# Weights of the third late gate requested inside the last scan; sample operands built before the last chunk

## The chip, the cores and the metric

The kernel runs on one core of one Trainium2 chip. The metric is the device time of one execution in microseconds. The core has a matrix engine (PE, with its own weight loads, PEld), a vector engine (DVE), an activation engine (ACT), a general engine (POOL) and a queue that issues transfers (SP). Each engine takes its instructions in a fixed order; they wait for each other by semaphores.

## The reference

One decoder layer on 1024 prompt tokens and 8 x 8 sample tokens, model width 1024, all in 32-bit floats. In short:

```python
h = rmsnorm(x, g_mix_pre) * (1 + scale_m) + shift_m
sc_b, sc_c, sc_x, z, xbc, dt_raw = split(h @ w_in)   # z: columns 3072..4095, the gates
y_sc = sc_b * causal_dwconv(sc_c * sc_x)             # short convolution
xs, Bm, Cm = split(silu(causal_dwconv(xbc)))
y_ssd, new_state = ssd_scan(xs, dt, A, Bm, Cm, d_skip, ssm_state)   # 4 groups of 4 heads
y_ssd = rmsnorm((y_ssd * silu(z)) per group) * ssm_norm_g
x = x + gate_m * rmsnorm(concat(y_sc, y_ssd) @ w_out)
x = x + gate_f * rmsnorm(swiglu(x))
```

The scan works on the prompt in chunks of 128 tokens with a state that is carried on. The 64 sample tokens start from a state given for each of their 8 sequences (state_ssm) and return a new one.

## The kernel before, in words

Every product is made of three: each operand is split into a high part (an ACT cast, `copy`) and a low part (a DVE subtraction), and high x high, high x low and low x high are summed (lines 332 to 334 in `acc3`). A weight block is loaded into a `raw` tile, split into `wh` and `wl`, and used as the stationary operand against the hidden rows `hh` (high) and `hl` (low) in three column chunks of 384, 384 and 320 tokens.

The mixer goes over the four groups g = 0..3. `ssd(g)` is a generator that makes the scan of a group in four double chunks: `part_a` (transposes, products B x C), `part_m` (decay factors), `part_b` (lines 739 to 769: products, the state S carried on DVE in lines 760 and 763, and the products with S in line 754). After the fourth it does the sample tokens: `sample_a` (factors), `sample_states` (load and transpose the given states, s0), `sample_b` (lines 810 to 822: the operands XS and BS of the state products), and, for the two head pairs, products from s0, the state products XS x BS (line 873), the update of s0 in place (lines 874 and 877), and its transfer out (line 878). `merge` interleaves a scan with side work: in scans 0 to 2 the input projections of the next group and the conditioning products, in scan 3 `gate` and `norm` of groups 0 and 1 (lines 888 and 901). The program order is only a priority: the compiler's scheduler lets later instructions run ahead when it thinks them ready, and fixes the order of each engine.

Behind the loop the memory on the left side is given up (`left.close()`, line 1092) and divided anew. The new pools lie on the old ones in this order: `rws` (4 raw tiles) on `rawp`, the first four tiles of `wsc` (weight parts) on `wp`, the other four and the sums `x56` on `fmp` (8 tiles of all 1088 tokens) and on `stp` (6 small tiles). A new tile waits for the old ones under it. `gate_late(2)` and `gate_late(3)` (line 1140) are the gates of groups 2 and 3, with weights from `plain_w` (lines 1009 to 1015 load and split). Between their chunks a generator `sums_h` makes the operand sums (lines 1117 to 1125, DVE) that the short-convolution projections (`sc_unit`, lines 1030 to 1070) need; `sums_last` follows. `raw_half` asks for weights in line 1010, the older `load_w` in line 301; both on SP. `y_out` (lines 935 and 936) sends finished rows out on SP too.

`rawp` has four tiles. In scan 3 they hold the two raw halves of gate 0, the two of gate 1, and then, in the first two again, s0 of the two head pairs.

Of the kernel before, what the change touches and what calls it, by code (L numbers as in the profile page):

```python
# [10 lines left out]
F32R = mybir.dt.float32r  # L11
# [5 lines left out]
P = 128  # L17
D = 1024
KT = 8
# [14 lines left out]
def hymba_step(ctx, tc, i, o):  # L34
# [7 lines left out]
    base, mid, left, right, banks = (ExitStack() for _ in range(5))  # L42

    def pool(stage, name, bufs, **kw):
        return stage.enter_context(tc.tile_pool(name=name, bufs=bufs, reuse_waits="tile", **kw))
# [21 lines left out]
    def fm(dt=F32):  # L67
        return fmp.tile([P, T], dt, tag="fm", name=nm("fm"))
# [8 lines left out]
    def st(shape, dt=F32):  # L77
        return stp.tile(shape, dt, tag="st", name=nm("st"))

    def gz(shape):  # L80
        return gzp.tile(shape, F32, tag="gz", name=nm("gz"))
# [39 lines left out]
    w_in = i["w_in"][0]  # L121
# [565 lines left out]
    def ssd(g, x0, x1, Bf, Cf):  # L687
# [4 lines left out]
        def part_a(j):  # L692
            cc = slice(2 * j, 2 * j + 2)
            col = 256 * j
            tpx, tpb = pz(), pz()
            for c in range(2):
                oc = col + c * P
                for p in range(2):
                    nc.tensor.transpose(tpx[:, c * 256 + p * P:c * 256 + (p + 1) * P], xc[p][:, oc:oc + P], ident)
                nc.tensor.transpose(tpb[:, c * P:(c + 1) * P], Bf[:, oc:oc + P], ident)  # L700
            for c in range(2):
                oc = col + c * P
                mm(tpb[:, 256 + c * P:256 + (c + 1) * P], Bf[:, oc:oc + P], Cf[:, oc:oc + P], start=True, stop=True)
            xd = st([P, 2, 2, 4, 64])
            for e, factor in enumerate((dt, edend)):
                nc.vector.tensor_tensor(xd[:, e], tpx.rearrange("p (c r q) -> p c r q", c=2, r=4),
                                        bc(factor[:, cc, hs], 3, 64), op=mult)
            bb = st([P, 2, 2, P])
            nc.scalar.copy(bb[:, 0].rearrange("p c n -> p (c n)"), tpb[:, :256])
            nc.vector.tensor_tensor(bb[:, 1], tpb[:, 256:].rearrange("p (c n) -> p c n", c=2),  # L710
                                    bc(ut, 1, 2), op=mult)
            return xd, bb
# [61 lines left out]
        def sample_a():  # L774
            tpx, tpb = pz(), pz()
            for p in range(2):
                nc.tensor.transpose(tpx[:NS, p * P:(p + 1) * P], xc[p][:, col:], ident)
            nc.tensor.transpose(tpb[:NS, 0:P], Bf[:, col:], ident)
            mm(tpb[:NS, P:P + NS], Bf[:, col:], Cf[:, col:], start=True, stop=True)
            ac = pz()  # L780
            for r in range(4):
                mm(ac[:, r * NS:(r + 1) * NS], sel(4 * g + r), acT[:, col:], start=True, stop=True)
            xd = st([NS, 2, 4, 64])
            for e, factor in enumerate((dt, edend)):
                nc.vector.tensor_tensor(xd[:, e], tpx[:NS, :256].rearrange("p (r q) -> p r q", r=4),
                                        bc(factor[:NS, 8, hs], 2, 64), op=mult)
            EC = st([P, 3, 4, NS])
            acv = ac[:, :256].rearrange("p (r l) -> p r l", r=4)
            E, Cx = EC[:NS, 0], EC[:, 1]
            nc.scalar.activation(Cx, acv, AF.Exp)  # L790
            nc.vector.tensor_tensor(E, acv[:NS], bc(acum[:NS, 8, hs], 2, NS), op=sub)
            nc.vector.tensor_scalar(E, E, 0.0, None, op0=mn)
            nc.scalar.activation(E, E, AF.Exp)
            CBm = EC[:NS, 2, 0, :]
            nc.vector.tensor_tensor(CBm, tpb[:NS, P:P + NS], utsf, op=mult)

            XB = gzp.tile([96, 768], F32R, tag="gz", name=nm("XB"))
            Bp = XB[:NS, 512:768].rearrange("k (j n) -> k j n", j=2)
            nc.scalar.copy(Bp[:, 0, :], tpb[:NS, 0:P])
            nc.vector.tensor_tensor(Bp[:, 1, :], tpb[:NS, 0:P], Bp[:, 0, :], op=sub)  # L800
            nc.vector.tensor_tensor(E, E, bc(CBm, 1, 4), op=mult)
            dsm = sp.tile([P, 2, 8], F32, tag="dsm", name=nm("dsm"))
            for p in range(2):
                for h in range(2):
                    nc.vector.tensor_copy(dsm[64 * h:64 * h + 64, p, :],
                                          bt(Cx[64 * h:64 * h + 64, 2 * p + h, :])[:, :, 7])
            nc.vector.tensor_tensor(Cx, Cx, bc(Cf[:, col:], 1, 4), op=mult)
            return xd, E, Cx, XB, Bp, dsm

        def sample_b(xd, XB, Bp):  # L810
            XS = XB[:, 0:512].rearrange("k (q m) -> k q m", q=2)
            BS = st([96, 2, 512], F32R)
            for q in range(2):
                own, other = slice(32 * q, 32 * q + 32), slice(32 - 32 * q, 64 - 32 * q)
                v = xd[own, 1].rearrange("k r q -> k (r q)")
                nc.scalar.copy(XS[own, q, :], v)
                nc.scalar.copy(XS[64:96, q, :], v)
                nc.vector.tensor_tensor(XS[other, q, :], v, XS[own, q, :], op=sub)
                for part, at in ((0, own), (0, other), (1, slice(64, 96))):
                    (nc.vector if part else nc.gpsimd).tensor_tensor(  # L820
                        BS[at, q, :].rearrange("k (b n) -> k b n", b=4), bc(Bp[own, part, :], 1, 4),
                        bc(blk4[own], 2, P), op=mult)
            return XS, BS

# [13 lines left out]
        m = part_m(0, *a)  # L838
        yield
        for j in range(4):  # L840
            a2 = part_a(j + 1) if j < 3 else sample_a()
            yield
            part_b(j, *a, *m)
            yield
            if j < 3:
                a = a2
                m = part_m(j + 1, *a)
                yield
        xd, E, Cx, XB, Bp, dsm = a2
        s0, s0T = sample_states(0)  # L850
        XS, BS = sample_b(xd, XB, Bp)
        yield
        S = state[0]
        fps = pz()
# [31 lines left out]
    def gate(g, y):  # L886
        ws = load_cols(w_in, 3072 + 256 * g, 2)
        for m in range(2):
            for c in range(3):
                proj_c(ws[m], hh, hl, gate_out(y[m]), c)  # L890
                yield
# [64 lines left out]
    def blend(a, b, na, nb):  # L956
# [4 lines left out]
        yield from a  # L961
        yield from b

    tl = [[] for _ in range(4)]
    run(group_tiles(0, tl[0]))
    for g in range(4):
        if g < 3:
            side = group_tiles(g + 1, tl[g + 1])
            if g > 0:
                side = blend(side, ada_steps(g), 12, 9)  # L970
        else:
            side = itertools.chain(*(f for h in range(2) for f in (
                gate(h, tl[h][:2]), norm(h, tl[h][:2], lambda: gz([P, 2, 384]), fm_row))))
        run(merge(ssd(g, *tl[g]), side, (0.67, 1.17, 1.17, 1.67)[g]))
    pre_scale("A_f", 4, gpre1)
    ys = [t[:2] for t in tl]
# [64 lines left out]
    def plain_w(w, cols):  # L1041
        raws = [raw_half(w, j, cols) for j in range(2)]
        W = {}
        for m in range(2):
            for j in range(2):
                t = in_turn(w_from).tile([P, 2, 4, P], F32R, tag="wc", name=nm("wp_"))
                part(t[:, 0], t[:, 1], raws[j][:, :, m * P:(m + 1) * P])
                W[m, j] = [[t[:, s, k] for k in range(4)] for s in range(2)]
        return W
# [40 lines left out]


    left.close()
    rws, wsc = pool(left, "rws", 4), pool(left, "wsc", 8)
    x56, x4 = pool(left, "x56", 8), pool(left, "x4", 4)
    pap, psx, psy = (pool(left, n, b) for n, b in (("pap", 2), ("psx", 1), ("psy", 1)))
    raw_from, w_from = [rws] * 4, [wsc] * 8

    X_sc = [{p: [] for p in (4, 5, 6)} for _ in SQ]
    X_t = {p: [] for p in (4, 5, 6)}
# [40 lines left out]
    def gate_late(g, y, W, between):  # L1140
        n_ = 0
        for m in range(2):
            w = [W[m, j][s][k] for s in range(2) for j in range(2) for k in range(4)]
            for c, (c0, n) in enumerate(CH):
                ps = pm()
                chained(acc3, ps, n, [(w[k], w[8 + k], hh[k][:, c0:c0 + n], hl[k][:, c0:c0 + n]) for k in range(KT)])
                gate_out(y[m])(ps, c, c0, n)
                for gen in between.get(n_, ()):
                    next(gen, None)
                n_ += 1  # L1150
# [6 lines left out]

    sums = sums_h()
    norm2, norm3 = (norm(g, ys[g], sq_row, sx_row) for g in (2, 3))
    gate_late(2, ys[2], plain_w(w_in, 3072 + 512), {n: [sums] for n in range(6)})  # L1160
    gate_late(3, ys[3], plain_w(w_in, 3072 + 768), {n: [sums] for n in range(6)})
    run(sums)
    sums_last()

# [560 lines left out]
```

## Time and profile before

| | us |
|---|---|
| median of 3 runs (1778.58 to 1783.43) | 1783.38 |
| the profiled execution | 1773.94 |
| its span | 1772.2 |
| PE busy in it | 1688.8 (95%) |
| DVE busy | 1174.1 (66%) |
| ACT busy | 778.6 (44%) |

A profile row gives times in microseconds from the span's start. A row of a timeline holds the start, the time taken by the run of like instructions, the engine, the line, the operation, output <- inputs, the shape and, in brackets, how long the engine was idle before it and what ended that. Matmuls are pipelined, so the rate of a stream of them is read from start to start. A row of a table of stretches holds the stretch and its length, then each engine's busy time with its count of instructions, the granted PE clock (1.00 is 2.4 GHz, 0.50 is 1.2 GHz), the busy share of the DMA engines and what they moved.

### The profile page before, as it was taken

Reading aid. Unit: us, or ns where it says so; the run is one execution under the profiler, and the core shown is the slowest. Engines: PE = TensorE matmul, PEld = TensorE weight load, DVE = VectorE, ACT = ScalarE, POOL = GpSimd, SP = SyncE. Lnnn points to the kernel's source line nnn. Section 1 sums busy time; section 2 is a strip of 40 time slices with the busy share of each in tenths; the row PEclk is TensorE's granted clock in tenths of the full one; section 3 lists DMA queues with packets and bytes.
Section 4 is the critical chain, followed back from the end, with each engine's and each line's share of the span. In section 5 each row is a group of like instructions: output and inputs, shape, how many; then the busy total and the mean of one; then the engine's idle time right before and its main releaser. Section 6 shows DMA issues by size and latency. Waiting matters only on the chain.

```text
span 1772.2 us, 31608 instructions
## 1 busy us (share of the span) xinstructions
PE 1688.8 (95%) x12624; PEld 1602.8 (90%) x12624; DVE 1174.1 (66%) x2263; ACT 778.6 (44%) x1597; POOL 237.6 (13%) x333
## 2 busy tenths in 40 slices
PE   5999999999699999999999899999999999899997
PEld 4998887889599899998989899999999999899987
DVE  5588777767867776660127769666665576677845
ACT  3456454558334333331226666444444455322303
POOL 2111021200000000000000000122222200322303
PEclk9999999999699999999999999999999999999999
DMA  9210435331502412348275634334434448856243
GB/s 316 70 36 25 129 119 177 119 122 52 172 25 87 149 50 98 115 137 301 84 247 181 195 115 147 120 137 148 147 137 152 146 151 311 324 213 236 99 152 119
DMA packets 160634, 259.74 MB, mean 147 GB/s; under 512 B 10561, under 2 KB 124401, under 8 KB 158182
## 3 DMA queue, kind: packets, MB, share of 16 engines
q1 hardware_dynamic: 160486, 257.71, 42.3%
q8 instruction: 99, 1.62, 0.4%
q14 instruction: 49, 0.40, 0.1%
HBM read 186.30 MB, written 71.38 MB: 145 GB/s over the span
## 4 chain that ended last, share of the span: by engine, by line
PE 82%; DVE 7%; DMA 3%; ACT 3%; issue 2%; POOL 1%; SPq 1%; DVEq 0%; POOLq 0%; ACTq 0%
PE pm L332 10%; PE pm L333 10%; PE pm L334 10%; PE pz L1055 7%; PE pz L1053 7%; PE pz L1054 7%; PE pm L1053 7%; PE pm L1055 7%; PE pm L1054 7%; DMA raw<-in_w_in 1%; PE pz L749 1%; PE pm L207 1%; PE pz L743 1%; PE pz L754 1%; PE pz L721 1%
## 5 line engine op out<-in xcount | busy, mean ns | idle before, releaser
L310 DVE TENSOR_TENSOR wl<-raw,wh 128x512 fp32r<-128x512 f32 (+1 forms) x83 | 59.0, 733 | 102.0 <-ACT wh L309 98.8
L334 PE MATMUL pm<-hb,wl 128*128 128x512 f32 (+2 forms) x320 | 108.3, 340 | 3.2 <-DVE wl L310 3.2
L333 PE MATMUL pm<-hb,wh 128*128 128x512 f32 (+2 forms) x320 | 108.1, 339 | 0.0
L332 PE MATMUL pm<-hb,wh 128*128 128x512 f32 (+2 forms) x320 | 106.8, 339 | 1.1 <-ACT wh L309 1.0
L333 PE MATMUL pm<-h,wh 128*128 128x384 f32 (+1 forms) x306 | 101.8, 333 | 0.0
L332 PE MATMUL pm<-h,wh 128*128 128x384 f32 (+1 forms) x306 | 101.5, 332 | 0.0
L334 PE MATMUL pm<-h,wl 128*128 128x384 f32 (+1 forms) x306 | 100.9, 331 | 0.0
L309 ACT CAST wh<-raw 128x512 fp32r<-128x512 f32 (+1 forms) x85 | 54.0, 667 | 106.1 <-PE pm L333 66.6
L1015 DVE TENSOR_TENSOR fs<-f,fs 128x512 fp32r<-128x512 f32 (+1 forms) x80 | 55.9, 711 | 27.5 <-ACT fs L1014 26.7
L334 PEld LDWEIGHTS pm<-hb,wl 128*128 128x128 f32 x320 | 61.2, 191 | 9.3 <-DVE wl L310 3.9
L1014 ACT CAST fs<-f 128x512 fp32r<-128x512 f32 (+1 forms) x80 | 46.7, 598 | 50.3 <-DMA f_d<-fs 33.0
L332 PEld LDWEIGHTS pm<-hb,wh 128*128 128x128 f32 x320 | 60.8, 191 | 7.0 <-ACT wh L309 1.6
L1070 DVE TENSOR_TENSOR facc<-facc,pz 128x288 f32<-128x288 f32 x124 | 55.9, 451 | 15.6 <-PE pz L1055 15.2
L333 PEld LDWEIGHTS pm<-hb,wh 128*128 128x128 f32 x320 | 61.1, 191 | 5.4
L332 PEld LDWEIGHTS pm<-h,wh 128*128 128x128 f32 x306 | 57.5, 188 | 1.3 <-issue 0.7
L333 PEld LDWEIGHTS pm<-h,wh 128*128 128x128 f32 x306 | 57.4, 188 | 1.0 <-issue 0.3
L334 PEld LDWEIGHTS pm<-h,wl 128*128 128x128 f32 x306 | 57.5, 188 | 0.9 <-issue 0.9
L1070 DVE TENSOR_TENSOR facc<-facc,pm 128x256 f32<-128x256 f32 x124 | 51.5, 415 | 5.7 <-PE pm L1055 4.5
L1032 POOL TENSOR_TENSOR raw<-raw 128x512 f32<-128x512 f32 x16 | 22.5, 1404 | 205.7 <-DVE raw L1030 205.7
L332 PE MATMUL pm<-bt,wh 128*128 128x384 f32 (+1 forms) x134 | 46.6, 347 | 0.0
L434 ACT COPY ext<-pm 128x384 f32<-128x384 f32 (+1 forms) x44 | 19.3, 445 | 57.9 <-PE pm L334 54.0
L333 PE MATMUL pm<-bt,wh 128*128 128x384 f32 (+1 forms) x134 | 43.7, 326 | 0.0
(7553 smaller groups left out, 6506.3 us busy)
## 6 DMA issues: line engine op xcount, KB each, us to landing
raw<-in_w_in SPq DMA_DIRECT2D x48, 512.0 KB
fc<-f_d SPq DMA_DIRECT2D x9, 2016.0 KB
f_d<-fs SPq DMA_DIRECT2D x31, 576.0 KB
wa<-in_w_ada SPq DMA_DIRECT2D x32, 512.0 KB
raw<-in_w_out SPq DMA_DIRECT2D x32, 512.0 KB
fc<-f_d SPq DMA_DIRECT2D x9, 1792.0 KB
f_d<-fs SPq DMA_DIRECT2D x31, 512.0 KB
raw<-in_w_gate SPq DMA_DIRECT2D x28, 512.0 KB
```

What stands on the lines that cost most here:

```text
L309: (nc.gpsimd.tensor_copy if hi_eng else nc.scalar.copy)(wh, raw)
L310: (eng or nc.vector).tensor_tensor(wl, raw, wh, op=sub)
L332: mm(ps[:, :n], wh, xh, start=(first and j == 0), stop=False)
L333: mm(ps[:, :n], wh, xl, start=False, stop=False)
L334: mm(ps[:, :n], wl, xh, start=False, stop=(last and j == end))
L1014: nc.scalar.copy(hi, v)
L1015: (eng or nc.vector).tensor_tensor(lo, v, hi, op=sub)
L1032: eng.tensor_tensor(a21, a11, a21, op=sub)
L1053: mm(ps, W[0][k], X[0][k], start=(start and k == 0), stop=False, skip_group_check=True)
L1054: mm(ps, W[0][k], X[1][k], start=False, stop=False, skip_group_check=True)
L1055: mm(ps, W[1][k], X[0][k], start=False, stop=(stop and k == nk - 1), skip_group_check=True)
L1070: nc.vector.tensor_tensor(out(q, i, h), out(q, i, h), ps, op=add)
```

## The change

In every scan the operands XS and BS of the sample tokens (`sample_b`) are built right behind `sample_a`, ahead of the fourth `part_b` instead of behind it, and BS lies in the `fm` pool instead of the `st` pool. In scan 3 a step `load_next` is put between the gate and the norm of group 1: it asks for the weights of the third gate, columns 3584 to 3839 of `w_in`, by `load_cols`, into two `raw` tiles and the two pairs `wh`, `wl` that the gates 0 and 1 use. `gate_late(2)` takes these. The eight tiles of `wsc` become two pools of four, and the ring of weight tiles now begins with the four on `fmp`; the fourth gate is the first to take from it.

```diff
@@ sample_b
-            BS = st([96, 2, 512], F32R)
+            BS = fm(F32R)[:96, :1024].rearrange("k (q n) -> k q n", q=2)
@@ ssd
-            a2 = part_a(j + 1) if j < 3 else sample_a()
+            if j < 3:
+                a2 = part_a(j + 1)
+            else:
+                a2 = sample_a()
+                XS, BS = sample_b(a2[0], *a2[3:5])
             yield
             part_b(j, *a, *m)
...
         s0, s0T = sample_states(0)
-        XS, BS = sample_b(xd, XB, Bp)
@@ the loop over the groups
+    w_next = []
+    def load_next():
+        w_next.extend(load_cols(w_in, 3072 + 512, 2))
+        yield
...
-            side = itertools.chain(*(f for h in range(2) for f in (
-                gate(h, tl[h][:2]), norm(h, tl[h][:2], lambda: gz([P, 2, 384]), fm_row))))
+            gates, norms = zip(*((gate(h, tl[h][:2]), norm(h, tl[h][:2], lambda: gz([P, 2, 384]), fm_row))
+                                 for h in range(2)))
+            side = itertools.chain(gates[0], norms[0], gates[1], load_next(), norms[1])
@@ behind left.close()
-    rws, wsc = pool(left, "rws", 4), pool(left, "wsc", 8)
+    rws, wsca, wscb = pool(left, "rws", 4), pool(left, "wsca", 4), pool(left, "wscb", 4)
-    raw_from, w_from = [rws] * 4, [wsc] * 8
+    raw_from, w_from = [rws] * 4, [wscb] * 4 + [wsca] * 4
@@ the late gates
-    gate_late(2, ys[2], plain_w(w_in, 3072 + 512), {n: [sums] for n in range(6)})
+    gate_late(2, ys[2], [[v[:, k] for v in w for k in range(KT)] for w in w_next], {n: [sums] for n in range(6)})
```

`gate_late(3)` keeps `plain_w`, with its list of parts now made by the caller.

## Rows read from the trace of the kernel before

**Rows 1.** The page: PE and its granted clock in 40 slices, in tenths.
```profile
PE   5999999999699999999999899999999999899997
PEclk9999999999699999999999999999999999999999
```

**Rows 2.** Table of stretches, end of scan 3 to the end of the late gates.
```profile
420.00:442.00 22.00, 22.00 (x171) 19.86 (x170) 17.50 (x38) 21.18 (x36) 4.00 (x4) 1.00 0.26 103
442.00:453.00 11.00, 10.39 (x112) 8.65 (x110) 7.68 (x16) 4.24 (x9) 0.46 (x2) 0.76 0.04 13
446.00:448.00 2.00, 2.00 (x21) 1.75 (x18) 1.90 (x4) 0.59 (x1) 0.00 (x0) 0.91 0.22 66
453.00:461.00 8.00, 5.03 (x20) 4.34 (x20) 5.71 (x18) 0.30 (x1) 0.00 (x0) 0.50 0.21 66
461.00:474.00 13.00, 0.00 (x0) 0.00 (x0) 12.98 (x16) 4.29 (x7) 0.00 (x0) 0.63 0.88 292
474.00:500.00 26.00, 25.96 (x144) 25.74 (x145) 25.32 (x38) 13.43 (x24) 0.00 (x0) 0.92 0.39 123
500.00:524.00 24.00, 24.00 (x147) 24.00 (x146) 9.70 (x17) 5.84 (x11) 0.00 (x0) 1.00 0.08 23
```

**Rows 3.** Waits of PE from 100 to 480: who for whom, total, times, longest.
```profile
PE pm L332 <- ACT wp__625_4819 L1014: 13.1, 1, 13.1
PE pz L873 <- DVE st L858: 4.4, 2, 2.2
PE pz L754 <- DVE S L763: 1.7, 1, 1.7
```

**Rows 4.** Chain that ended last, from 461 to 474: start, length, what.
```profile
461.12 1.21 DVE s L877 x2
462.35 4.12 DMA out_ssm_s<-s
466.52 6.82 DMA raw<-in_w_in
```

**Rows 5.** Timeline of SP, from 371 to 422: its issues in scan 3.
```profile
371.58 6.11 SPq L827 DMA_DIRECT2D s<-in_state_ssm  x2
421.77 1.34 SPq L935 DMA_DIRECT2D y_d<-nr  x2
```

**Rows 6.** Timeline of PE: the same matmuls at full and at half clock.
```profile
413.57 0.83 PE L289 MATMUL pz<-ident,sm 128*128 128x128 f32 x6
455.90 4.18 PE L289 MATMUL pz<-ident,sm 128*128 128x128 f32 x18 [2.97 <-DVE sm L283]
```

**Rows 7.** Timeline of ACT and DVE: the fourth gate's splits, and the last operand sum.
```profile
477.80 0.62 ACT L1014 CAST wp__654_5038<-raw 128x512 fp32r<-128x512 f32 x1 [0.70 <-DMA raw<-in_w_in]
480.47 0.68 DVE L1015 TENSOR_TENSOR wp__654_5038<-raw,wp__654_5038 128x512 fp32r<-128x512 f32 x1
535.62 0.72 DVE L1015 TENSOR_TENSOR h<-t,h 128x544 fp32r<-128x544 f32 x1
```

**Rows 8.** Timelines of ACT, DVE, POOL, PE in scan 1: XS, BS and their user.
```profile
249.55 0.40 ACT L816 CAST XB<-st 32x256 fp32r<-32x256 f32 x1
254.85 0.84 DVE L818 TENSOR_TENSOR XB<-st,XB 32x256 fp32r<-32x256 f32 x2
257.91 5.80 POOL L820 TENSOR_TENSOR st<-XB,blk 32x512 fp32r<-32x512 f32 x3
262.75 1.05 DVE L427 SCALAR_TENSOR_TENSOR fm<-ext,vT,fm 128x64 f32<-128x64 f32 x1
266.01 1.38 DVE L820 TENSOR_TENSOR st<-XB,blk 32x512 fp32r<-32x512 f32 x2
267.99 0.47 PE L873 MATMUL pz<-st,XB 96*128 96x512 f32 x1 [2.22 <-DVE st L858]
```

**Rows 9.** Timeline of DVE in scan 3: the state's update without and beside POOL.
```profile
427.82 0.42 DVE L760 TENSOR_TENSOR S<-S,ecd 128x256 f32<-128x256 f32 x1
438.15 0.98 DVE L760 TENSOR_TENSOR S<-S,ecd 128x256 f32<-128x256 f32 x1 [0.58 <-PE pz L754]
```

More of the change, by code (lines that the diff above doesn't have):

```diff
@@ L1142, in gate_late @@
         for m in range(2):
-            w = [W[m, j][s][k] for s in range(2) for j in range(2) for k in range(4)]
+            w = W[m]
             for c, (c0, n) in enumerate(CH):
@@ L1159, in hymba_step @@
     norm2, norm3 = (norm(g, ys[g], sq_row, sx_row) for g in (2, 3))
-    gate_late(2, ys[2], plain_w(w_in, 3072 + 512), {n: [sums] for n in range(6)})
-    gate_late(3, ys[3], plain_w(w_in, 3072 + 768), {n: [sums] for n in range(6)})
+    gate_late(2, ys[2], [[v[:, k] for v in w for k in range(KT)] for w in w_next], {n: [sums] for n in range(6)})
+    W = plain_w(w_in, 3072 + 768)
+    gate_late(3, ys[3], [[W[m, j][s][k] for s in range(2) for j in range(2) for k in range(4)] for m in range(2)],
+              {n: [sums] for n in range(6)})
     run(sums)
```

## The prediction

> **What bounds the kernel now.** Read the slices first [rows 1]: PE is busy nine tenths or more nearly everywhere, so PE bounds the kernel, and time is to be had only where PE stands still or runs at half clock. One slice in the middle shows 6 on both lines, and it is the place of the change. The table of stretches resolves it [rows 2]: PE is full up to 442 (22.00 of 22.00), then idle for 0.61 us up to 453, 2.97 up to 461 and 13.00 up to 474, and nearly full behind it (25.96 of 26.00). That is 16.6 us, and from 446 on the clock falls to 1.2 GHz. The table of PE's waits names the causes [rows 3]: 13.1 us for the first split weights of the third gate, and 4.4 us in two pieces for the state products of the sample tokens (line 873). The chain gives the first wait its history [rows 4]: the last update of s0 ends at 462.3, its transfer out takes 4.12 us, and only then is the weight request issued, which lands 6.82 us later. So the weights wait for a memory slot: their raw tile lies on s0 of the second head pair.
>
> **The weights, step by step.** The new request goes into raw tiles that gate 0 and gate 1 leave, and s0 of the second pair moves to the last raw half of gate 1. In SP's order these three issues stand between the loads of s0 at 371 and the first transfer of `y_out` at 421 [rows 5], 44 us in which SP only waits: neither the request nor s0, whose user comes behind 442, is late, and nothing is held behind them. The parts lie in `wh` and `wl`: the first half is free when gate 1's first half has been multiplied, the second when PE ends gate 1 at 442. In work nothing is added: four casts, four subtractions and two transfers of 512 KB leave `plain_w` and come back in `load_cols`. Where they go matters. The first half's two casts (2 x 0.62 us) and two subtractions (2 x 0.68 us) [rows 7] fall into 420 to 442, where ACT is busy 21.18 of 22 us and DVE 17.50 [rows 2]. So I expect that half at about 445. This suffices, because PE has the transposes and small products of the tail to do from 442 on.
>
> Between 442 and the end of the third gate PE then does the same work without the holes. Idle time removed: 0.61 + 2.97 + 13.00 = 16.6 us [rows 2]. Clock: the 18 matmuls of line 289 take 4.18 us at half clock against 3 x 0.8 = 2.4 for three sixes at full clock, 1.8 us [rows 6]; the 144 matmuls of the third gate take 25.96 us, at the rate of the fourth gate (24.00 / 147 = 0.163 us) they take 23.5, another 2.4 us [rows 2]. The ceiling is 16.6 + 1.8 + 2.4 = 20.8 us. From it I take 3 us for what I can't see: about 1.2 for the two casts in the full ACT stretch, the rest for an order of PE that is fixed ahead and doesn't meet the real moments. Term: **-17.8 us**. Its bounds: the ceiling of 20.8, and 13.1 [rows 3] if PE's order leaves the tail as it is and only the wait goes.
>
> **What is late next.** The fourth gate would start at about 480 instead of 500. The second quarter of its parts is cast by 478.4 and subtracted by 481.2 now [rows 7], behind the third gate's four splits, which no longer stand there (4 x 0.6 = 2.4 us): 479, so no wait. Its raw tiles now lie on s0 of the first pair and on the early weights, both done before s0 of the second pair. Then DVE: it is busy 7.68 + 5.71 + 12.98 + 25.32 = 51.7 of 58 us from 442 to 500, then 9.70 of 24 [rows 2], and the last operand sum of the next projection ends at 535.62 + 0.72 = 536.3 [rows 7]. Of the 61.4 us of DVE work between 442 and the fourth gate's end at 524, some 4 (splits and parts of `sample_b`) move ahead of 442; 57 us must fit into the 62 us up to 504. It fits with about 5 us to spare; so no term of its own, but a loss of up to 8 us is kept as a rival.
>
> **The operands, step by step.** In scan 1 POOL's multiplications of BS begin at 257.9 and DVE's two only at 266.0, behind the whole convolution of the next group's tile, so PE waits 2.22 us for line 873 [rows 8]; the second piece of the 4.4 us is the same in scan 2 [rows 3]. XS is ready at 255.7. Built behind `sample_a`, ahead of `part_b`, all of it is done some 10 us sooner, and PE is next held there by nothing that the rows show: -4.4 us. Against it: DVE's four instructions (0.84 + 1.38 = 2.2 us) and ACT's four casts (4 x 0.40 = 1.6 us) [rows 8] now stand in front of `part_b`, with its state updates queued behind DVE's. In scan 0, where line 754 already waits 1.7 us for the state [rows 3], I take 1 us more (bounds 0 and 2.2); in the others PE has projections at hand, so 0 (bound 2.2 each). BS in `fm` gives a small tile back to the chunk loop and takes one of eight large ones: in scan 3 the others are acT, the tiles of B and C, two y tiles and two norm rows, eight of eight; the y tiles and rows go free with the transfers of 421 [rows 5], long before norm 1 wants rows. I cost it at nothing; the cover is gone if those transfers are late. Term: -4.4 + 1.0 = **-3.4 us**, bounds -4.4 and 4 x 2.2 - 4.4 = +4.4.
>
> POOL and DVE disturb each other here: the state update of line 760 takes 0.42 us alone and 0.98 while POOL builds BS [rows 9]. The Trainium skill (SBUF — State Buffer, section "SBUF: two separate sides") gives a reason: a GpSimd instruction and a DVE instruction with two SBUF inputs take the same port pair by an exclusive lock, and the later one stands still. It speaks against this change, which puts more of POOL's work beside the state updates; the row at 438.15 agrees. By it, three more updates stretched by 0.56 us in each of four scans would cost 6.7 us if PE always waited for them, and the second term would turn to +3.3.
>
> **The sum.** -17.8 - 3.4 = -21.2 us against the profiled execution's 1773.94 gives 1752.7. That execution is 9.4 us below the median of the runs shown, so against the median of 1783.38 the forecast is **1762.2 us**. Differences under 0.3% (5.3 us) can't be told from no change.
>
> **Rivals.**
> *PE's order stays.* The third gate's products are queued behind the tail, because the order was fixed with the weights thought late; only the 13.1 us go: 1783.4 - 13.1 - 3.4 = 1766.9. For it: the order is fixed ahead. Against: nothing of the tail feeds these products. Chance 0.14.
> *DVE becomes the bound.* The sums end up to 8 us late, seen as idle PE at 505 to 520: 1770.2. For it: 51.7 of 58 us busy [rows 2]. Against: from 500 to 524 it has 14 us free. Chance 0.14.
> *The change doesn't do what it says.* The wait moves to the fourth gate: its request stays behind the transfers of `y_out` in SP's order and lands a whole landing of 6.8 us [rows 4] behind the 481 of now, 2 us of which were to spare at best: 1762.2 + 6.8 + 2 = 1771. Chance 0.05.
> *No change: the clock.* It began to fall from 446 to 448 while PE was busy 2.00 of 2.00 us with small products [rows 2]. If it stays at 1.2 GHz for the whole third gate, that takes 23.5 us more than at full clock: 1783.4 - 16.6 - 2.4 + 23.5 - 3.4 = 1784.5. Against: from 420 to 442, where the chunk's small products stand among full ones, it is 1.00. Chance 0.05.
> *Slower.* The pulled-up operands hold the state chain: `part_b` stands behind POOL's run of 5.8 us and the 2.2 + 1.6 us of DVE and ACT [rows 8], 9.6 us in each of four scans, 38.4 us: 1783.4 - 17.8 - 4.4 + 38.4 = 1799.6. It decides from 22.2 / 4 = 5.6 us a scan. Against: `part_b` reads nothing that POOL makes, and PE has side work. Chance 0.05.
> The forecast itself holds 0.57.
>
> **How the numbers follow.** Faster by over 0.3%: 0.57 + 0.14 + 0.14 + 0.05 = 0.90, less 0.05 for the spread of the runs (1778.58 to 1783.43): 0.85. Slower by over 0.3%: 0.05, and 0.01 for the spread: 0.06. Within: 0.09. The range goes from the ceiling, 1783.4 - 20.8 - 4.4 = 1758.2, less 3.7 of spread, 1754.5, to the latest of the faster rivals, 1771, plus 4.5, 1775.5.
>
> **What will show it.** Right: no wait of line 332 for split weights at 461 to 474; the third gate's matmuls stand among lines 832, 867 and 906 from about 445; the fourth gate starts near 480; the clock stays near 1.00; the two waits of line 873 are gone; the instruction counts of DVE and ACT are unchanged. Wrong: idle PE ahead of the fourth gate (its weights), at 505 to 520 (DVE) or at line 754 (the state chain); a clock of 0.50 through the third gate. The prediction fails as a whole if PE's idle time in the chunk loop grows by more than what the end of scan 3 loses.

## The result, and the profile after

| | before | after |
|---|---|---|
| median of 4 runs each, side by side (us) | 1783.37 | 1763.29 |
| range of the runs (us) | 1778.58 to 1783.43 | 1760.32 to 1764.89 |
| ratio, 95% interval | | 0.9892 (0.987 to 0.9914) |
| the profiled execution (us) | 1773.94 | 1764.2 |
| its span (us) | 1772.2 | 1762.5 |

The forecast was 1762.2 us (0.9881 of before), and the time fell on it. The two profiled executions differ by only 9.7 us, though, where the sum said 21.2. A second comparison of the same two kernels, below, gave 0.992 (0.9896 to 0.9944). The first question is therefore where the expected gain stands in the trace, and where it is lost again. Of all timed runs below one, of v_pool, is left out as a slow execution (2057.96 us at a granted clock of 0.749).

Table of stretches of the kernel after, over the same stretches as [rows 2], then one longer stretch. Columns as there: the stretch and its length, busy time of PE, PEld, DVE, ACT, POOL, granted clock, share and rate of the DMA engines.

```profile
442.00:453.00 11.00, 9.62 (x89) 8.99 (x90) 8.75 (x17) 4.82 (x10) 0.15 (x1) 0.84 0.04 12
453.00:461.00 8.00, 8.00 (x59) 6.67 (x59) 3.36 (x10) 1.17 (x2) 0.00 (x0) 0.63 0.22 66
461.00:474.00 13.00, 13.00 (x83) 12.62 (x82) 9.72 (x20) 3.42 (x5) 0.00 (x0) 0.97 0.30 104
474.00:500.00 26.00, 25.09 (x150) 24.56 (x149) 25.62 (x37) 11.83 (x22) 0.00 (x0) 1.00 0.54 177
500.00:524.00 24.00, 23.57 (x168) 23.18 (x166) 23.65 (x41) 11.67 (x23) 0.00 (x0) 1.00 0.15 44
...
470.00:526.00 56.00, 54.14 (x353) 53.19 (x352) 55.26 (x84) 27.30 (x51) 0.00 (x0) 1.00 0.39 125
```

The hole of 13.00 us is gone. Two things took part of its place. PE is full from 453 to 461 but at a granted clock of 0.63. And DVE is busy 55.26 of 56.00 us from 470 to 526: it has become the engine that is never free.

Waits of PE in the kernel after, in all and longest, first from 100 to 480, then from 480 to 660 (lines 754, 763 and 289 are the old ones; 1024 and 1025 are the old 1014 and 1015, 1063 to 1065 the old 1053 to 1055, 1078 the old 1068, 1127 the old 1117).

```profile
PE pz L754 <- DVE S L763: 4.5, 2, 2.8
...
PE pm L1063 <- ACT y L1078: 1.9, 1, 1.9
PE pz L289 <- DVE sm L283: 1.4, 1, 1.4
PE pm L1065 <- DVE w__726_5815 L1025: 0.9, 1, 0.9
PE pm L334 <- DVE wp__653_5038 L1025: 0.9, 1, 0.9
PE pm L1064 <- DVE h L1025: 0.5, 1, 0.5
PE pm L1063 <- ACT h L1024: 0.4, 1, 0.4
```

Of [rows 3] the 13.1 us and the 4.4 us are gone. The wait for the state (line 754) grew from 1.7 to 4.5 us: 2.8 in scan 0, where it was 1.7, and a new one of 1.7 in scan 3 (at 443.4). Behind 480 the kernel before has only these two:

```profile
PE pm L1053 <- ACT y L1068: 2.2, 2, 1.8
PE pz L289 <- DVE sm L283: 1.4, 1, 1.4
```

So the first two rows behind 480 are old. New are the four others, of 0.4 to 0.9 us, three of which end with a low half from DVE.

To place the difference, the same matmul is looked up in both traces, and its starts are compared:

| from, to | forecast (us) | measured (us) |
|---|---|---|
| start of the span, scan 0 reached | 0 | +3.1 |
| scan 0 | +1.0 | +2.6 |
| scans 1 and 2 | -4.4 | -4.7 |
| scan 3, up to the fourth gate's first product | -17.8 | -16.4 |
| fourth gate and first six projection units | 0 | +5.5 |
| the rest, to the end | 0 | +0.1 |
| sum | -21.2 | -9.7 |

The third and fourth lines are nearly right. The loss behind the fourth gate's start is the step that the sum lacked. From scan 0 on, start to start, this pair of traces gains 12.8 us.

For every kernel below two stretches are read: scan 3's start to the fourth gate's first product, and from there to the seventh projection unit. PE's idle time is the length less PE's busy time. The cost of the clock is the sum, over 48 equal slices of a stretch, of PE's busy time times one less the granted clock.

| kernel | first stretch | idle | clock | second stretch | idle | clock |
|---|---|---|---|---|---|---|
| before | 131.78 | 16.62 | 7.23 | 163.43 | 3.57 | 0.00 |
| after | 115.34 | 1.71 | 5.09 | 168.91 | 6.42 | 1.71 |
| after_again | 115.43 | 1.71 | 5.12 | 168.96 | 6.47 | 1.60 |
| weights_only | 115.44 | 0.73 | 6.81 | 173.78 | 9.93 | 2.98 |
| fm_late | 112.94 | 1.70 | 3.41 | 174.56 | 9.19 | 4.91 |
| early12 | 110.88 | 0.75 | 1.71 | 175.16 | 10.08 | 4.45 |
| v_act | 115.23 | 1.77 | 5.14 | 166.25 | 4.73 | 1.39 |
| v_pool | 115.16 | 1.78 | 5.11 | 171.59 | 9.40 | 2.15 |
| early123 | 112.45 | 1.77 | 1.71 | 169.19 | 6.65 | 1.52 |
| early123_again | 115.12 | 1.71 | 5.11 | 167.79 | 6.80 | 0.00 |
| low_pool | 110.80 | 1.71 | 0.00 | 172.60 | 8.98 | 2.70 |

What is left when idle time and clock are taken off is the same work in all of them: 107.8 to 109.1 us in the first stretch, 159.8 to 161.0 in the second. So the difference between these kernels in the two stretches is, to within 1.3 us in each, PE's idle time and PE's clock.

### The profile page after: what moved, and what is told of

Its sections match the earlier page's. It is cut to its first block, busy times and chain, and to the rows that moved or that the text cites. A ratio compares the mean times of both kernels' runs of the same rounds, so it can differ in the third digit from the quotient of the medians.

```text
span 1762.5 us, 31586 instructions
## 1 busy us (share of the span) xinstructions
PE 1693.1 (96%) x12624; PEld 1605.9 (91%) x12624; DVE 1173.0 (67%) x2263; ACT 773.5 (44%) x1595; POOL 231.8 (13%) x333
## 5 line engine op out<-in xcount | busy, mean ns | idle before, releaser
L333 PE MATMUL pm<-h,wh 128*128 128x384 f32 (+1 forms) x342 | 115.2, 337 | 0.0
L332 PE MATMUL pm<-h,wh 128*128 128x384 f32 (+1 forms) x342 | 115.1, 337 | 0.0
L334 PE MATMUL pm<-h,wl 128*128 128x384 f32 (+1 forms) x342 | 114.4, 336 | 0.0
L332 PEld LDWEIGHTS pm<-h,wh 128*128 128x128 f32 x342 | 65.5, 192 | 1.9 <-issue 1.0
L1080 DVE TENSOR_TENSOR facc<-facc,pz 128x288 f32<-128x288 f32 x124 | 55.9, 451 | 16.7 <-PE pz L1065 16.4
L333 PEld LDWEIGHTS pm<-h,wh 128*128 128x128 f32 x342 | 65.4, 191 | 1.1 <-issue 0.3
L334 PEld LDWEIGHTS pm<-h,wl 128*128 128x128 f32 x342 | 65.4, 191 | 0.9 <-issue 0.9
L332 PE MATMUL pm<-bt,wh 128*128 128x384 f32 (+1 forms) x146 | 51.4, 352 | 0.0
L334 PE MATMUL pm<-bt,wl 128*128 128x384 f32 (+1 forms) x146 | 48.5, 332 | 0.3 <-DVE wl L310 0.2
L333 PE MATMUL pm<-bt,wh 128*128 128x384 f32 (+1 forms) x146 | 48.1, 330 | 0.0
```

Source lines behind the costliest of these rows:

```text
L332: mm(ps[:, :n], wh, xh, start=(first and j == 0), stop=False)
L333: mm(ps[:, :n], wh, xl, start=False, stop=False)
L334: mm(ps[:, :n], wl, xh, start=False, stop=(last and j == end))
L1080: nc.vector.tensor_tensor(out(q, i, h), out(q, i, h), ps, op=add)
```

## The experiments

Three sets were run, each beside its own runs of the kernel before, whose medians were 1776.52 (14 runs), 1780.72 (13) and 1777.52 us (9); times of different sets are compared by their ratio to these. A trace is one execution, and not always a typical one: after_again, early12 and v_act were profiled in the slowest of their runs, early123, fm_late and low_pool in the fastest.

**The two kernels again.** No edit.

> The kernel before, unchanged, for a second profile. The first profiled execution took 1773.94 us, below every timed run (1778.58 to 1783.43). If executions differ by what the transfers at the start do, the second profile differs from the first by up to 8 us and mostly before 100 us of the span; the end of scan 3 should repeat: a PE wait of about 13 us for the third gate's split weights, two waits of 2.2 us in line 873. If the first profile was typical, the second lies within 2 us of it.

> The changed kernel, unchanged, for a second profile and more times. First profile 1764.2 us. Ratio 0.988 to 0.990. If the 3.2 us that the first profile was late before scan 0 are chance, they differ here; the 2.6 us lost in scan 0, the 4.6 us won in scans 1 and 2, and the 15 us won at the end of scan 3 should repeat within 0.5 us.

Measured: before 1776.98 us, span 1775.3; after 1761.74 us (1757.69 to 1765.59), span 1763.9, ratio 0.992 (0.9896 to 0.9944). Against the first trace of before, scan 0's +2.6, the -4.7 in scans 1 and 2 and the end of scan 3 (-16.4) repeat to within 0.2 us. The second trace of before differs in scan 1, which takes 89.6 us instead of 88.1: behind the 2.2 us wait of line 873 its granted clock falls, and it does so in other_slots too. A stretch of before_again:

```profile
268.00:272.20 4.20, 4.20 (x16) 4.07 (x15) 3.27 (x4) 0.00 (x0) 0.00 (x0) 0.59 0.54 156
```

By the measure of the table above this costs 1.7 us, so the waits that the early operands remove are sometimes worth more than their length. Scan 0 is reached between 0.2 us earlier and 4.6 us later than in the first trace, also by kernels whose code is the same up to there (112.5 to 116.5 us in after, after_again, v_act and v_pool); the +3.1 us are therefore put down to chance. The gain is 0.8 to 1.1% by two comparisons, and of before's runs 1783.4 was a high median.

**The weights alone.** The operands as before, the rest of the change kept.

```diff
-            BS = fm(F32R)[:96, :1024].rearrange("k (q n) -> k q n", q=2)
+            BS = st([96, 2, 512], F32R)
...
-                XS, BS = sample_b(a2[0], *a2[3:5])
...
+        XS, BS = sample_b(xd, XB, Bp)
```

> The early request alone; the operands of the sample tokens stay behind the last chunk and BS in the small pool. Theory: the request brings nearly the whole gain at the end of scan 3, and the pulled-up operands hurt there, because the state update queues behind them on DVE (PE waits 1.7 us for it in the changed kernel). Then the end of scan 3 wins 16 to 18 us, scan 0 loses nothing, the two waits of 2.2 us in line 873 stay: 15 to 18 us in all, ratio 0.990 to 0.991. Rival: the products can only run ahead when the operands are early too; then it wins 13 us at most at the end of scan 3, ratio 0.993 or more.

Measured: 1768.88 us (1765.74 to 1771.84), ratio 0.9952 (0.9929 to 0.9975). The theory's 16 to 18 us at the end of scan 3 are there (-16.3 by starts), but 10.35 of them are given back in the second stretch. The time is the rival's, though not by the rival's reason, since the products do run ahead. PE's waits from 480 to 560:

```profile
PE pm L334 <- DVE wp__653_5038 L1025: 3.7, 1, 3.7
PE pm L1063 <- ACT h L1024: 1.3, 1, 1.3
PE pm L1064 <- DVE h L1025: 0.4, 1, 0.4
```

Two stretches of the same kernel:

```profile
487.00:490.00 3.00, 0.00 (x0) 0.00 (x0) 2.27 (x5) 3.00 (x7) 0.00 (x0) 1.00 0.21 66
490.00:494.00 4.00, 3.61 (x12) 3.61 (x13) 4.00 (x7) 1.18 (x3) 0.00 (x0) 0.60 0.14 20
```

PE stands for the fourth gate's first low half, and then runs at 0.60: here a wait is paid for twice, once as idle time and once by the clock behind it.

**The operands alone.** An edit of the kernel before.

```diff
-            BS = st([96, 2, 512], F32R)
+            BS = fm(F32R)[:96, :1024].rearrange("k (q n) -> k q n", q=2)
...
-            a2 = part_a(j + 1) if j < 3 else sample_a()
+            if j < 3:
+                a2 = part_a(j + 1)
+            else:
+                a2 = sample_a()
+                XS, BS = sample_b(a2[0], *a2[3:5])
...
-        XS, BS = sample_b(xd, XB, Bp)
```

> The operands ahead of the last chunk and BS in the large pool, in all four scans, without the early request. Theory: +2.6 us in scan 0, -2.2 us each in scans 1 and 2, about 0 to +2 at the end of scan 3 where the wait for the weights hides it: -2 to 0 us in all, ratio 0.999 to 1.000. Rival (the forecast's own term): -3.4 us and more in scan 3 through the earlier state products, ratio 0.996 to 0.998.

Measured: 1775.74 us (1771.26 to 1781.9), ratio 0.9992 (0.9973 to 1.001): no difference that can be measured. By starts scan 0 loses 2.6 us and scans 1 and 2 gain 4.4, -1.8 in sum; some 0.4 us of that is drift at the start of scan 2. The third gate still waits 13.5 us. This is as the theory had it.

**Early operands in scans 1 to 3, not in scan 0.**

```diff
-            BS = fm(F32R)[:96, :1024].rearrange("k (q n) -> k q n", q=2)
+            BS = (fm(F32R)[:96, :1024].rearrange("k (q n) -> k q n", q=2) if g in (1, 2, 3) else
+                  st([96, 2, 512], F32R))
...
-                XS, BS = sample_b(a2[0], *a2[3:5])
+                if g in (1, 2, 3):
+                    XS, BS = sample_b(a2[0], *a2[3:5])
...
+        if g not in (1, 2, 3):
+            XS, BS = sample_b(xd, XB, Bp)
```

> The changed kernel, but the sample tokens' operands are made ahead of the last chunk only in scans 1, 2 and 3 (in scan 0 behind it, in their old buffer). Theory (in scan 0 the early operands stand in DVE's queue ahead of the state sum of line 763 and cost 2.5 us): the first chunk of scan 1 starts as early as in the kernel with the weights alone, the gains of 2.45 us in scans 1 and 2 stay, so the whole is 2.5 us better than the changed kernel: ratio about 0.9905. Rival (scan 0 loses through something else that the change brings, such as the other buffer): no gain over the changed kernel, ratio 0.992.

Measured: 1757.8 us (1757.47 to 1762.54), ratio 0.9884 (0.9842 to 0.9925). Scan 0's loss is gone (0.0 us by starts) and the gains of scans 1 and 2 stay. Timeline of DVE in scan 0, first the kernel after, then (last row) early123:

```profile
174.20 1.17 DVE L801 TENSOR_TENSOR st<-st 64x256 f32<-64x256 f32 x1
...
175.71 0.68 DVE L820 TENSOR_TENSOR fm<-XB,blk 32x512 fp32r<-32x512 f32 x1
176.87 0.68 DVE L820 TENSOR_TENSOR fm<-XB,blk 32x512 fp32r<-32x512 f32 x1
177.59 0.42 DVE L763 TENSOR_TENSOR S<-S,pz 128x256 f32<-128x256 f32 x1
```

```profile
173.00 0.42 DVE L763 TENSOR_TENSOR S<-S,pz 128x256 f32<-128x256 f32 x1
```

In the kernel after, the state's sum of line 763 stands behind all of `sample_b`'s work on DVE; in early123 it runs 3.6 us sooner, counted from the update of line 760 ahead of it (at 168.46 and 167.49), and PE waits for it 1.7 us instead of 2.8. That is 1.1 us of the 2.6. The rest is PE's clock. The 4 us behind the wait, first in the kernel after, then (last row) in early123:

```profile
178.00:182.00 4.00, 3.94 (x18) 3.69 (x19) 4.00 (x9) 0.00 (x0) 0.00 (x0) 0.57 0.01 2
```

```profile
173.40:177.40 4.00, 3.93 (x45) 3.52 (x45) 3.94 (x10) 0.97 (x4) 0.62 (x1) 1.00 0.00 0
```

Over scan 0 the clock costs 1.7 us in after, after_again, operands_only and v_act and 6.5 in v_pool, all with the wait of 2.8 us. Of the nine traces in which that wait is 1.5 to 1.7 us, it costs 1.7 us in two (early12, low_pool) and nothing in seven.

**Is it the new buffer or the early place?** The kernel after, with BS in `fm`, but `sample_b` called behind the last chunk again; and early operands only in scans 1 and 2, with scan 3 as in weights_only (first edit fm_late, second early12).

```diff
-                XS, BS = sample_b(a2[0], *a2[3:5])
...
+        XS, BS = sample_b(xd, XB, Bp)
```

> The changed kernel, with the operands' low half in its new buffer but made behind the last chunk, where they stood before. Theory (the early place makes scans 1 and 2 faster, and in scan 3 it is the old buffer, shared with what the sums behind it need, that costs the kernel with the weights alone 5 us more behind the fourth gate's start): scans 0 to 2 as before (0, 0, 0 us), the sums' first instruction on line 1127 near 470 us as in the changed kernel, loss behind the fourth gate's start about 5.5 us, ratio about 0.993. Rival (the place in the queue decides there too): sums start near 473.5, loss near 10 us, ratio 0.995.

Measured: 1769.51 us (1763.69 to 1772.78), ratio 0.9938 (0.9917 to 0.996). The theory's early sums are there (first one at 468.0 us), but the loss in the second stretch is 11.1 us, as the rival had it. So the buffer lets the sums start sooner, and that doesn't help.

```diff
-            BS = fm(F32R)[:96, :1024].rearrange("k (q n) -> k q n", q=2)
+            BS = (fm(F32R)[:96, :1024].rearrange("k (q n) -> k q n", q=2) if g in (1, 2) else
+                  st([96, 2, 512], F32R))
...
-                XS, BS = sample_b(a2[0], *a2[3:5])
+                if g in (1, 2):
+                    XS, BS = sample_b(a2[0], *a2[3:5])
...
+        if g not in (1, 2):
+            XS, BS = sample_b(xd, XB, Bp)
```

> The operands early, with their new buffer, only in scans 1 and 2; scans 0 and 3 as in the kernel with the weights alone. Theory (the early place in scan 3 is worth nothing up to the fourth gate's start but keeps VectorE's line shorter behind it): gains of 2.45 us in scans 1 and 2, none and no loss in scan 0, from the fourth gate's start on a loss of 10 us as in the kernel with the weights alone: end some 5 us better than that kernel, ratio 0.9925. Rival (what costs the kernel with the weights alone its 5 us is chance of its clock): loss of 5.5 to 6 us, ratio 0.990.

Measured: 1760.21 us (1759.25 to 1763.74), ratio 0.9901 (0.9888 to 0.9915). In the trace the loss in the second stretch is 11.7 us, as the theory had it, and the profiled execution also has the theory's time (1763.74 us, 0.992). It is the slowest of the four, though; the median is the rival's, and the three faster runs have no trace. The first stretch shows what can differ: there the clock took 1.71 us here and 6.81 in weights_only, whose scan 3 is the same. The wait for the first low half, longest, in fm_late (first row) and in early12:

```profile
PE pm L334 <- DVE wp__653_5038 L1025: 2.6, 1, 2.6
```

```profile
PE pm L334 <- DVE wp__653_5038 L1029: 3.7, 1, 3.7
```

With late operands in scan 3 this wait is 2.6 to 3.7 us in three kernels, with early ones 0.9 to 1.0 in after, early123 and its repetition, and the idle time of the second stretch is 9.2 to 10.1 against 6.4 to 6.8. So the early place in scan 3 is worth some 3 us there, by keeping DVE less far behind PE, although it moves nothing up to the fourth gate. There BS in `fm` even costs something: in all traces with that buffer in scan 3, fm_late too, PE waits 1.7 to 1.8 us for the state (line 754) between 438 and 446, and in weights_only and early12 it doesn't. Why the order that the compiler then gives DVE is shorter wasn't traced instruction by instruction.

**Is it DVE?** The eight additions of line 1127 (1.29 us each) become copies on ScalarE, or go to GpSimd.

```diff
-                nc.vector.tensor_tensor(v[j], hh[k + 4 * j], hl[k + 4 * j], op=add)
+                nc.scalar.copy(v[j], hh[k + 4 * j])
```

> The changed kernel with VectorE's eight additions of line 1127 (8 x 1.29 us, at 470 to 498 us) replaced by eight copies on ScalarE, which leave the low halves out of the sums. Theory (VectorE has no gap from 470 to 526 us, and this is what gives 5.5 us of the gain back behind the fourth gate's start): of the 5.5 us at least 4 come back, 1 us before the first product behind the gate and the rest in the first units, ratio about 0.9895. Rival (the given-back time is TensorE's own, by its clock or its order): unchanged within 1 us, ratio 0.992.

Measured: 1758.03 us (1755.81 to 1759.79), ratio 0.9876 (0.9842 to 0.991). The same long stretch as above:

```profile
470.00:526.00 56.00, 56.00 (x376) 56.00 (x375) 48.17 (x79) 32.04 (x57) 0.00 (x0) 1.00 0.39 125
```

PE is busy 56.00 of 56.00 us: with 7 us less on DVE, its idle time there (1.86 us in the kernel after) is gone. Of the 5.5 us that were given back, 2.7 return, less than the theory's 4 and more than the rival's 1. What stays is mainly a wait of 0.9 us for another low half (line 1065) and the clock's 1.4 us behind the wait for line 1078. The kernel before has that last wait too (1.8 us), at its line 1068, without a fall of the clock, so this part isn't shown to come from DVE.

```diff
-                nc.vector.tensor_tensor(v[j], hh[k + 4 * j], hl[k + 4 * j], op=add)
+                nc.gpsimd.tensor_tensor(v[j], hh[k + 4 * j], hl[k + 4 * j], op=add)
```

> The changed kernel with the same eight additions of line 1127 moved to GpSimd, which stands idle from 454 to 539 us; each should take about 2.5 us there (estimate from 2.36 us for a 128x1024 of line 310). Theory (VectorE decides, GpSimd is free): most of what the kernel with the copies gains is gained, ratio 0.990. Rival (GpSimd's work slows VectorE's beside it, as 0.42 became 0.98 us in rows 9, or the first sums wait for it): no gain or a loss, ratio 0.992 to 0.994.

Measured: 1766.35 us (1763.97 to 1767.66, five runs), ratio 0.9918 (0.9891 to 0.9945). The rival: the loss of the second stretch grows from 5.5 to 8.2 us. (The 6.5 us of clock in its scan 0 lie outside the edit.) Timeline of POOL:

```profile
479.75 2.96 POOL L1127 TENSOR_TENSOR y<-h,h 128x1088 f32<-128x1088 f32 x1 [5.83 <-DVE x__630_4861 L1025]
484.70 5.79 POOL L1127 TENSOR_TENSOR y<-h,h 128x1088 f32<-128x1088 f32 x2 [2.00 <-DVE y L1132]
```

Timeline of DVE beside it:

```profile
480.69 2.59 DVE L1135 TENSOR_TENSOR y<-y 128x544 f32<-128x544 f32 x1
485.27 2.88 DVE L1025 TENSOR_TENSOR x__635_4866<-y,x__635_4866 128x544 fp32r<-128x544 f32 x1
```

PE's longest wait:

```profile
PE pm L334 <- DVE wp__653_5038 L1025: 4.8, 1, 4.8
```

DVE's 128x544 subtractions take 0.72 us alone (line 1129 and the like in the kernel after), and 2.59 and 2.88 beside a sum on POOL: they begin while POOL's sum runs, and end about 0.6 us behind it. POOL was idle, and yet its work was not free.

**Only the four low halves on GpSimd.** On top of early123.

```diff
-    def plain_w(w, cols):
+    def plain_w(w, cols, eng=None):
...
-                part(t[:, 0], t[:, 1], raws[j][:, :, m * P:(m + 1) * P])
+                part(t[:, 0], t[:, 1], raws[j][:, :, m * P:(m + 1) * P], eng)
...
-    W = plain_w(w_in, 3072 + 768)
+    W = plain_w(w_in, 3072 + 768, nc.gpsimd)
```

> early123 with the four low halves of the fourth gate's weights (4 x 0.69 us of VectorE near 479 to 484 us) subtracted by GpSimd, idle then, about 1.4 us each (1.40 for a 128x512 of line 1042 in the changed kernel). Theory (VectorE without a gap decides behind the fourth gate's start): TensorE's wait of 1.0 us for the first low half goes, and 2.8 us of VectorE's line are saved, of which some 1 to 2 us show: 1.5 to 2.5 us better than early123, ratio 0.987 to 0.9875. Rival (GpSimd beside VectorE slows both, as with the eight additions): the wait stays or grows, no gain, 0.9885 or more.

Measured: 1764.18 us (1758.74 to 1765.18), ratio 0.9913 (0.9898 to 0.9927). PE's waits from 480 to 560:

```profile
PE pm L1067 <- ACT h L1028: 3.4, 1, 3.4
PE pm L1068 <- DVE h L1029: 1.1, 2, 0.7
```

Timelines, the first of POOL's four instructions:

```profile
474.68 1.74 POOL L1029 TENSOR_TENSOR wp__653_5038<-raw,wp__653_5038 128x512 fp32r<-128x512 f32 x1 [29.00 <-ACT wp__653_5038 L1028]
```

and DVE's additions, of 1.28 us when alone, the first of them just ahead of it:

```profile
473.98 1.29 DVE L1131 TENSOR_TENSOR y<-h,h 128x1088 f32<-128x1088 f32 x1
...
480.41 2.38 DVE L1131 TENSOR_TENSOR y<-h,h 128x1088 f32<-128x1088 f32 x1
```

A stretch, with DVE busy all of it:

```profile
474.00:500.00 26.00, 26.00 (x160) 26.00 (x159) 26.00 (x34) 11.79 (x23) 6.95 (x4) 1.00 0.25 75
```

POOL's first instruction begins while DVE's addition runs (to 475.26) and ends 1.16 us behind it; so each engine holds the other up. The wait ahead of the fourth gate is gone, as the theory had it, and more than it comes back as 3.4 us in the first projection unit, behind DVE's sums: PE's idle time in the second stretch is 8.98 us against 6.65. That is the rival's result by its mechanism, at another place.

**early123 again.** No edit.

> The same kernel as early123 a second time, to see whether its end of scan 3 repeats. There the clock stayed at 1.00 from 445 to 475 us of its span, while the changed kernel, with the same instructions in the same order on TensorE, fell to 0.50 from 455 to 462 and lost 3.4 us by it. Theory (the clock's second fall hangs on when this kernel arrives there, and repeats with the kernel): no second fall, fourth gate near 478 us from the span's start, ratio 0.988 to 0.989. Rival (chance of one execution): the fall is back, fourth gate near 481.5, ratio 0.990.

Measured: 1756.68 us (1754.21 to 1761.37), ratio 0.9885 (0.9868 to 0.9902). Stretches around the same matmuls, first early123, then its repetition:

```profile
450.00:458.00 8.00, 8.00 (x73) 7.16 (x72) 4.68 (x16) 1.11 (x3) 0.00 (x0) 1.00 0.22 68
```

```profile
447.00:455.00 8.00, 8.00 (x55) 6.52 (x54) 3.37 (x10) 0.65 (x2) 0.00 (x0) 0.53 0.20 62
```

The fall is back, so the rival is right there: the same instructions in the same order run at 1.00 in one execution and at 0.53 in another, and 3.4 us hang on it (5.11 against 1.71 in the table). The time holds (0.9884 and 0.9885). That this kernel beats the change is shown by its traces, where scan 0 takes 2.6 us less; by times it lies below after_again's 0.992, but it can't be told from the first comparison's 0.9892.

**What did the weights wait for?** The kernel before, with the third gate's raw weights on the two raw tiles that are not s0 of the second pair.

```diff
-    rws, wsc = pool(left, "rws", 4), pool(left, "wsc", 8)
+    rwsa, rwsb, wsc = pool(left, "rwsa", 2), pool(left, "rwsb", 2), pool(left, "wsc", 8)
-    raw_from, w_from = [rws] * 4, [wsc] * 8
+    raw_from, w_from = [rwsb] * 2 + [rwsa] * 2, [wsc] * 8
```

> The kernel before, with the third gate's raw weights in the two raw tiles that do not lie on s0 of the second head pair, so that their request need not wait until that state is written out; the order of SyncE's queue is the same. Theory (the prediction's: the weights wait for the memory slot): the wait of 13.1 us for line 332 shrinks by the 4.1 us of the transfer or more. Rival (the request stands in SyncE's queue behind the last transfers of y_out, whose last issue ends at 466.4 us, where the slot came free at 466.5): the request stays at 466.4, the wait changes by under 0.3 us, ratio 1.000.

Measured: 1777.69 us, a single run. PE's wait:

```profile
PE pm L332 <- ACT wp__625_4822 L1014: 13.1, 1, 13.1
```

Timeline of SP, first the kernel before, then this one:

```profile
465.24 1.17 SPq L936 DMA_DIRECT2D y_d<-y  x1
```

```profile
466.26 1.16 SPq L935 DMA_DIRECT2D y_d<-nr  x1
467.51 1.19 SPq L936 DMA_DIRECT2D y_d<-y  x1
468.80 11.35 SPq L1010 DMA_DIRECT2D raw<-in_w_in  x6
```

The wait is 13.1 us as before, and the request follows directly on the last transfer of `y_out` (this execution runs 2.2 us late as a whole). The rival: a free slot alone brings nothing, since the request is also last in SP's queue. In the kernel before the two locks opened within 0.1 us of each other, the queue at 466.41 and the slot at 466.47 [rows 4], and the chain of waits names only one. That the slot alone would hold the weights as long is read from these two numbers; no run frees the queue alone.

## Why the prediction was right, and where its steps failed

**The place and the mechanism were right.** The request goes out at 378.49, the first half's last low part is ready at 445.98 (expected: about 445), the third gate's products stand among the transposes and small products of the tail from 447.49 on, and the two waits of line 873 are gone. So the rival in which PE's order stays is out. The instruction count of DVE stays at 2263, ACT's is 1595 against 1597.

**The cause was half right.** The slot on s0 was one lock of two (other_slots). The change opens both, since its request is also far ahead of the transfers in SP's order; a smaller edit that moved only the slot would have been forecast wrongly.

**The weights' term, -17.8, measured -16.4 up to the fourth gate.** The idle time went nearly as counted, 16.62 to 1.71 us; the 1.71 are the new wait for the state in scan 3. The clock did not: 4.2 us of it were to come back, and 2.1 came (7.23 to 5.09). "The clock stays near 1.00" was the wrong step. Timeline of PE in the kernel after:

```profile
447.49 0.67 PE L332 MATMUL pm<-bt,wh 128*128 128x384 f32 x1
450.66 1.10 PE L870 MATMUL pz<-st,st 128*64 128x8 f32 x32
...
458.90 0.52 PE L332 MATMUL pm<-h,wh 128*128 128x384 f32 x1
461.99 0.34 PE L333 MATMUL pm<-h,wh 128*128 128x384 f32 x1
```

A matmul of the same shape takes 0.52 us at 458.90 and 0.34 at 461.99. The prediction's evidence was the chunk loop from 420 to 442, where the clock is 1.00; but it had also seen the fall between 446 and 448 with PE busy 2.00 of 2.00 [rows 2], and put it aside. The rival that put the clock at 1.2 GHz through the whole third gate was too dark: 5.1 us and not 23.5.

**"DVE fits with about 5 us to spare" was the step that failed.** It counted 57 us of DVE's work into the 62 us up to 504. The work runs up to the last operand sum, which ended 12 us behind the fourth gate's end even before (536.3 against 524), and those 12 us, 12.1 of them busy, were left out; and from 442 to 474 DVE stands idle for 10.2 of 32 us in the kernel after, because its work there waits for results of PE, mostly directly or by way of ACT. Measured from 442 to the last sum: 71.6 us busy of 82.5. Rows of the kernel after, DVE's first sum, the fourth gate's first low half, and the last sum:

```profile
470.15 1.28 DVE L1127 TENSOR_TENSOR y<-bt,bt 128x1088 f32<-128x1088 f32 x1
485.34 0.69 DVE L1025 TENSOR_TENSOR wp__653_5038<-raw,wp__653_5038 128x512 fp32r<-128x512 f32 x1
523.79 0.71 DVE L1025 TENSOR_TENSOR h<-t,h 128x544 fp32r<-128x544 f32 x1
```

and SP's request for that gate:

```profile
474.27 16.30 SPq L1020 DMA_DIRECT2D raw<-in_w_in  x6
```

The rival "DVE becomes the bound" was therefore no alternative to the forecast: its mechanism came true beside it. Of its 8 us 5.5 were lost: 2.85 are more idle time, 1.71 the clock, and the rest is in neither. v_act shows that about half hangs on DVE's work; the clock's part isn't shown to. The rival that moved the wait to the fourth gate came true in part: its request does stand behind `y_out` (474.27, and not early as hoped). But the high half is cast by 482.3, and the low half begins only at 485.34, 3.0 us later, behind other work in DVE's queue; PE waits 0.9 us. In v_act the request goes out at 474.78, no earlier, and this wait is gone, so it was DVE's queue and not the request.

**The operands' term, -3.4, measured -2.0 (after) and -1.8 (operands_only).** The two waits were priced right (-4.7 and -4.4, each with 0.2 to 0.4 of drift). Scan 0 cost 2.6 us, over the upper bound of 2.2. The wait itself grew by 1.1 us, close to the 1.0 that was taken, although the state's sum came 3.6 us later on DVE: the compiler put lines 801 and 807 of `sample_a` ahead of it as well. What the term lacked is the clock behind that wait, 1.7 us. In scan 3 the term had nothing; there the buffer in `fm` brings the wait of 1.7 us for the state, and the early place keeps some 3 us of idle time away behind it.

**The port lock.** POOL beside the state updates was to cost up to 6.7 us, an estimate from the lock that the Trainium skill states (SBUF — State Buffer, section "SBUF: two separate sides"). In the kernel after no update of line 760 takes over 0.43 us, so it costs nothing there. Other runs agree with the rule, by which the engine that starts second stands still: DVE in v_pool, where 0.72 us become 2.88, and POOL in low_pool, whose first 1.74 us end 1.16 us behind the addition that was running.

**The level was partly luck.** A sum of -21.2 was set against a median that later runs of before put 3 to 7 us lower, and the difference of medians is 14.8 to 20.1 us in the two comparisons. The first pair of traces, from scan 0 on, gains 12.8 us and the second 16.2 (its trace of before has the fall of the clock in scan 1). So by the traces the sum was 5 to 8 us too large, and that the time still fell within 1.1 us of the forecast owes much to the high runs of before.

## What to carry to other kernels

When a hole in the bound engine is filled, the next engine in line loses the same time to catch up: count its work not to the point where it was done before, but to the last result that the following stage reads, and subtract the time in which it can't work because it waits for the very stage that was sped up. Before moving a request, ask for everything that holds it, the slot and the queue, since the chain shows only the one that opened last. Price a wait by its length and also by the clock behind it, which in scan 0 added 1.7 us to a wait that grew by 1.1. And an early operand is worth its place only where the bound engine has other work: here three scans gained and one lost, so in the traces making it per scan beat making it everywhere.

## What the runs showed of the hardware

- The clock falls to 1.2 GHz with PE busy 8.00 of 8.00 us, among transposes and products of 8 columns, and it need not: the same order of instructions ran at 1.00 (early123) and at 0.53 (its repetition). Such a fall cost 3.4 us. Behind waits of about 2 us it fell in some executions, for up to 1.7 us more (after, at 598), and not in others (early123_again). Behind the wait of scan 0 it fell in five traces of five at 2.8 us, and in two of nine at 1.5 to 1.7 us.
- POOL's 128x1088 sums of 2.96 and 2.87 us stretched DVE's 128x544 from 0.72 to 2.59 and 2.88 us. Moving 10.3 us of DVE's work to an idle POOL lost 2.7 us in the second stretch.
